# Feed-forward of a two-block layer: five column groups instead of four, the last by token halves, and the context norm moved

## The chip, the cores and the metric

The program runs on one core of one Trainium2 chip. The metric is the device time of one execution in microseconds; three executions of the kernel before gave 4265.05, 4266.02 and 4270.29 us (median 4266.02).

## The reference, cut to what matters

Two blocks follow each other on 1024 tokens of width 1024; a context of 256 tokens joins in the second. Around the change stand the end of the first block and the start of the second (everything in float32):

```
h2 = layer_norm(x) * (1 + scale2) + shift2
u = h2 @ w_up                                   # 1024 x 5632
up = pad(u, two tokens in front)
u = conv_b + sum(conv_w[t] * up[:, t:t + S] for t in range(3))
u_gate, u_val = split(u, 2)                     # 2816 each
f = gelu(u_gate) * u_val
x = layer_norm(ALPHA * x + gate2 * (f @ w_down)) * ln2_g + ln2_b
...
# second block, first layer
n_l = rmsnorm(x, norm_w) * (1 + scale) + shift          # 1024 tokens
n_c = rmsnorm(ctx, norm_w) * (1 + scale_c) + shift_c    # 256 context tokens
y_l, y_c = even_layer(n_l, n_c, ...)                    # begins with n_l, n_c @ w_in
```

The convolution runs along the tokens, so a token needs the two tokens before it.

## The kernel before, in words

Every float32 matrix product is made of three passes over a high and a low part of both factors: `mm3` (L215) issues the three matmuls of lines 217, 218 and 219. Activations with channels in partitions are held as a pair of tiles `hhi`, `hlo` (`alloc_hT`, L221): index 0 holds tokens 0 to 511, index 1 tokens 512 to 1023, index 2 the context. There is one buffer for each index, so a new tile of index 0 can be written only when all readers of the old one are done.

`ffn` (L694) walks over 22 column tiles of 128 hidden channels in four groups of 6, 6, 6 and 4 (L703). For each group, `up` (L710) takes two tiles at a time: it loads the two 256-column slices of `w_up` (gate and value) with `wcols` (L180, split into high and low by ScalarE and VectorE, L176 and L177; two raw buffers, three of high and low each), and for each tile and half accumulates both token halves into a two-bank PSUM tile `p2` (two buffers). ScalarE (L731) and VectorE (L732, L734) convolve 1024 tokens at once, ScalarE applies gelu, GpSimd multiplies (L741), ScalarE and VectorE split the product into `fh` and `fl` (L742, L743). `down` (L746) multiplies the group's tiles by `w_down` for a token tile of 128 and half of the output columns, into PSUM tiles `pj` and `pt` in turn (two of each here, set by `open_ps(2)` at L632). For the first three groups the sum so far is kept in DRAM: for each of 16 (column half, token tile) items a 256 KB piece `xl` is loaded (two buffers), VectorE multiplies by the gate (L770) and adds (L771), and SyncE's queue stores it (L773).

The last group is different (L776 to L805). All of its `up` comes first; then both halves of `w_down`, multiplied by the gate on GpSimd (L173); then for each of the 8 token tiles: load the sum so far into `x2t` (L789, four buffers), two products and adds (L792), layer norm (L794: VectorE statistics, GpSimd power, ScalarE scale), times `ln2_g` on GpSimd (L795), plus `ln2_b` on VectorE (L796), store to DRAM (L803), root-mean-square norm (L804), and `to_hT` (L805, L364), which transposes the tile by TensorE into a `p2` tile and applies scale and shift from there, `ta` (7) of 8 slices on ScalarE (L387), the rest on VectorE (L389), then casts (L390) and subtracts (L391) into `nT[0]` or `nT[1]`. Tiles 6 and 7 take two VectorE operations (L801, L802) in place of L794 to L796.

`ctx_norm` (L1039) then does the same norm for two tiles of the context, writes `nT[2]`, and stores `nT[1]` and `nT[2]` to DRAM for later. `rw_prep1` (L1084) goes on with products of all three token sets with `even_w_in`: `fm_psum` (L1057) accumulates tokens 0 to 511, then 512 to 1023, in one `p2` tile, then the context in a `pj` tile. From here on weights are loaded on SyncE's queue (L1089).

The order of the instructions on each engine is not written by hand: a planner at build time walks over the program with simulated times, takes the earliest written instruction that is ready, and gives out buffers as they come free. On the chip each engine, and each DMA queue, works strictly in that order. All scratch pools stack on one side of the on-chip memory, so a pool opened after another was closed takes over its place and its waits.

## Time and profile before

| | us |
|---|---|
| three timed executions, median (lowest to highest) | 4266.02 (4265.05 to 4270.29) |
| the profiled execution, its own time | 4259.52 |
| its span in the trace | 4257.7 |
| TensorE busy in the span | 3895.7 (91%) |
| VectorE / ScalarE / GpSimd busy | 1964.8 / 1402.8 / 1133.4 |
| mean granted TensorE clock | 0.928 of full speed |

PE is TensorE, PEld its weight loads, DVE VectorE, ACT ScalarE, POOL GpSimd, SP SyncE; an engine's name with a q behind it is its queue of DMA issues. Times in a row count from the start of the span. In rows of the timeline the first number is the start, the second the duration (several merged ones together where the end says xN), and what stands in brackets is the idle time before it and what ended it. Busy times of PE overlap a little from one matmul to the next, so the distance of starts is the better measure of a matmul's price.

### The profile page before, as it was taken

How to read it: one execution, taken by the hardware profiler on the slowest of the kernel's cores; microseconds unless marked ns; L12 is line 12 of the kernel's file. 1: busy time of each engine (PE TensorE's matmuls, PEld its weight loads, DVE VectorE, ACT ScalarE, POOL GpSimd, SP SyncE). 2: the span in 40 equal slices, each digit the busy share in tenths (PEclk: the TensorE clock that was granted, in tenths of full speed). 3: DMA queues.
4: the chain of work that ended last, by engine and by line, in shares of the span. 5: the costliest groups of instructions: out<-in, count | busy, mean ns of one | idle time of the engine just before them, and what ended most of it. 6: DMA issues, size and time to landing. Idle time of an engine off the chain costs nothing. (4 is left out here: it accounts for less than half of the span.)

```text
span 4257.7 us, 62518 instructions
## 1 busy us (share of the span) xinstructions
PE 3895.7 (91%) x24873; PEld 3154.0 (74%) x24873; DVE 1964.8 (46%) x2944; ACT 1402.8 (33%) x2881; POOL 1133.4 (27%) x1135
## 2 busy tenths in 40 slices
PE   7999999988999999789879899988789999998987
PEld 4788877776878788567777787777567877776776
DVE  4232433447343434544235445443566426653576
ACT  4333322215212122442235444353224224432211
POOL 1110302223101011202265333226530200003574
PEclk9999979998999999878989899896789999998998
DMA  5321217573142413332476645553764644324465
GB/s 200 122 95 68 92 58 258 198 271 123 52 138 70 144 54 125 121 133 115 145 245 174 184 135 153 174 155 96 237 203 143 228 135 116 104 73 152 153 200 201
DMA packets 474212, 622.00 MB, mean 146 GB/s; under 512 B 163201, under 2 KB 324403, under 8 KB 467776
## 3 DMA queue, kind: packets, MB, share of 16 engines
q1 hardware_dynamic: 423440, 416.26, 30.4%
q0 software_dynamic: 50480, 201.75, 14.3%
q8 instruction: 196, 3.21, 0.3%
q14 instruction: 96, 0.79, 0.1%
HBM read 423.34 MB, written 193.88 MB: 145 GB/s over the span
## 5 line engine op out<-in xcount | busy, mean ns | idle before, releaser
L217 PE MATMUL p<-hhi,whi 128*128 128x512 f32 x1056 | 416.1, 395 | 5.8 <-DVE hf L389 5.7
L218 PE MATMUL p<-hlo,whi 128*128 128x512 f32 x1056 | 414.3, 392 | 4.3 <-DVE hlo L391 4.3
L219 PE MATMUL p<-hhi,wlo 128*128 128x512 f32 x1056 | 414.1, 392 | 0.0
L217 PE MATMUL pf<-whi,hhi 128*128 128x512 f32 (+1 forms) x992 | 357.7, 362 | 16.8 <-DMA whi<-wkh 6.9
L218 PE MATMUL pf<-wlo,hhi 128*128 128x512 f32 (+1 forms) x992 | 352.7, 356 | 7.9 <-POOL wlo L177 4.9
L219 PE MATMUL pf<-whi,hlo 128*128 128x512 f32 (+1 forms) x992 | 350.4, 354 | 0.0
L176 ACT CAST whi<-wraw 128x2048 fp32r<-128x2048 f32 (+1 forms) x123 | 193.1, 1574 | 463.4 <-PE pt L219 174.8
L177 DVE TENSOR_TENSOR wlo<-wraw,whi 128x2048 fp32r<-128x2048 f32 (+1 forms) x103 | 213.0, 2069 | 275.5 <-ACT whi L176 275.4
L217 PE MATMUL pf<-hhi,whi 128*128 128x512 f32 (+1 forms) x640 | 252.2, 394 | 3.8 <-ACT hyo L2050 1.5
L219 PE MATMUL pf<-hhi,wlo 128*128 128x512 f32 (+1 forms) x640 | 249.7, 390 | 1.8 <-DMA wlo<-wkl 1.8
L218 PE MATMUL pf<-hlo,whi 128*128 128x512 f32 (+1 forms) x640 | 249.8, 390 | 0.0
L217 PEld LDWEIGHTS p<-hhi,whi 128*128 128x128 f32 x1056 | 200.6, 190 | 53.8 <-DVE hf L389 6.1
L217 PEld LDWEIGHTS pf<-whi,hhi 128*128 128x128 f32 x992 | 198.2, 200 | 54.5 <-issue 12.4
L218 PEld LDWEIGHTS p<-hlo,whi 128*128 128x128 f32 x1056 | 200.3, 190 | 46.4 <-DVE hlo L391 5.3
L217 PE MATMUL pj<-whi,hhi 128*128 128x512 f32 (+1 forms) x560 | 216.2, 388 | 19.9 <-ACT whi L176 12.2
L219 PEld LDWEIGHTS p<-hhi,wlo 128*128 128x128 f32 x1056 | 200.1, 189 | 42.8 <-issue 0.8
L219 PE MATMUL pj<-whi,hlo 128*128 128x512 f32 (+1 forms) x560 | 214.2, 384 | 11.2 <-DVE hlo L381 11.2
L218 PEld LDWEIGHTS pf<-wlo,hhi 128*128 128x128 f32 x992 | 198.6, 200 | 34.2 <-POOL wlo L177 5.8
L218 PE MATMUL pj<-wlo,hhi 128*128 128x512 f32 (+1 forms) x560 | 214.9, 384 | 0.3 <-DVE wlo L177 0.3
L219 PEld LDWEIGHTS pf<-whi,hlo 128*128 128x128 f32 x992 | 197.8, 200 | 23.3 <-issue 2.3
L217 PEld LDWEIGHTS pf<-hhi,whi 128*128 128x128 f32 x640 | 122.3, 191 | 35.7 <-issue 9.3
L218 PEld LDWEIGHTS pf<-hlo,whi 128*128 128x128 f32 x640 | 122.2, 191 | 28.9 <-issue 6.9
(762 smaller groups left out, 8677.1 us busy)
## 6 DMA issues: line engine op xcount, KB each, us to landing
wraw<-w_in POOLq DMA_DIRECT2D x25, 1024.0 KB, 5.7
wraw<-w_ada POOLq DMA_DIRECT2D x24, 1024.0 KB, 8.0
wraw<-w_up POOLq DMA_DIRECT2D x22, 1024.0 KB, 6.0
whi<-wkh POOLq DMA_DIRECT2D x40, 512.0 KB, 4.9
wlo<-wkl POOLq DMA_DIRECT2D x40, 512.0 KB, 4.8
wraw<-ada_w POOLq DMA_DIRECT2D x32, 512.0 KB, 4.6
ox<-x SPq DMA_DIRECT2D x48, 256.0 KB
xp<-xl SPq DMA_DIRECT2D x48, 256.0 KB
```

Of the source, the lines that this page charges most:

```text
L176: nc.scalar.copy(hi[:, :n], raw[:, :n])
L177: self.we.tensor_sub(lo[:, :n], raw[:, :n], hi[:, :n].bitcast(F32))
L217: mm(out, L[0], R[0], start=first, stop=False)
L218: mm(out, L[0], R[1], start=False, stop=False)
L219: mm(out, L[1], R[0], start=False, stop=last)
```

## The change

The groups become 6, 6, 4, 4 and 2. The last group of two tiles no longer uses `up` and `down`: it goes through the tokens in two halves, and does for each half all of up, convolution (512 tokens at a time; the last two tokens of the first half are kept in `ends`), down, norms and transposes before the next. The first half's up goes into `p2` tiles, the second's into `pj` (gate) and `pt` (value). `w_down`'s two tiles of rows come as one gated piece of 1024 columns. `ta` is 5 from here on, so three of eight slices go to VectorE. The context norm stands in the fourth group, between its up and its down, writes its result to DRAM, and a new `ctx_load` reads it back where `ctx_norm` stood, and stores `nT[1]`.

```diff
--- before.py
+++ after.py
@@ -700,7 +700,7 @@
         self.nw2 = self.cols_of([a["norm_w_2"][0], a["norm_w_2"][1]], 8, "nw2")
         self.x2_d = [dr.tile([P, D], F32, name=f"x2_{t}") for t in TL]
         self.mod_e = None
-        groups = [(0, 6), (6, 6), (12, 6), (18, 4)]
+        groups = [(0, 6), (6, 6), (12, 4), (16, 4), (20, 2)]
         with ExitStack() as es:
             cp = es.enter_context(self.pool("ffc"))
             cw = self.cols_of([a["conv_w"][0], a["conv_w"][1], a["conv_w"][2], a["conv_b"]], 44, "cvw", cp)
@@ -759,6 +759,8 @@
                     dst = [dr.tile([P, D], F32, name=f"xp{gi}_{t}") for t in TL]
                     with self.pool(f"fff{gi}") as fp, self.pool(f"ffu{gi}") as p:
                         up(p, fp, fs, j0, n)
+                        if gi == 3:
+                            self.ctx_norm()
                         for c in range(2):
                             cs = slice(512 * c, 512 * c + 512)
                             W = self.wcols(w_down, 512 * c, 512, nk=n, k0=j0)
@@ -773,36 +775,78 @@
                                 nc.sync.dma_start(dst[t][:, cs], xl)
                     src = dst
                     continue
-                fp = es.enter_context(self.pool("fffl"))
-                with self.pool(f"ffu{gi}") as p:
-                    up(p, fp, fs, j0, n)
-                with self.pool("ffl") as p:
+                Wg = self.wcols(w_up, j0 * P, 256)
+                Wv = self.wcols(w_up, 2816 + j0 * P, 256)
+                W = self.wcols(w_down, 0, 1024, nk=n, k0=j0, gate=gate2)
+                with self.pool("fffl") as fp, self.pool("ffl") as p:
+                    ends = fp.tile([P, 2, 2, 2], F32, name="fce")
                     g1 = p.tile([P, D], F32, name="ln2g")
                     nc.sync.dma_start(g1, bcast_rows(a["ln2_g"], D))
                     b1 = p.tile([P, D], F32, name="ln2b")
                     nc.sync.dma_start(b1, bcast_rows(a["ln2_b"], D))
-                    W = [self.wcols(w_down, 512 * c, 512, nk=n, k0=j0, gate=gate2[:, 512 * c:512 * c + 512]) for c in range(2)]
-                    nT = [self.alloc_hT(0), self.alloc_hT(1)]
-                    for t in TL:
-                        xx = p.tile([P, D], F32, name="x2t", tag="x2t", bufs=4)
-                        nc.sync.dma_start(xx, src[t])
-                        for c in range(2):
-                            cs = slice(512 * c, 512 * c + 512)
-                            nc.vector.tensor_add(xx[:, cs], xx[:, cs], down(fs, W[c], t, n))
-                        ...
+                    nT = [None, None]
+                    self.ta = 5
+                    for b in range(2):
+                        fs = []
+                        for e in range(2):
+                            ts = []
+                            ps = self.p2() if b == 0 else None
+                            for half, Wu in ((0, Wg), (1, Wv)):
+                                u = ps[:, 512 * half:512 * half + 512] if b == 0 else (self.pt if half else self.pj)()
+                                for k in range(KD):
+                                    wk = (Wu[k][0][:, e * P:e * P + P], Wu[k][1][:, e * P:e * P + P])
+                                    self.mm3(u, wk, (h2T[b][0][:, k, :], h2T[b][1][:, k, :]), k == 0, k == KD - 1)
+                                jj = j0 + e + 22 * half
+                                w = lambda i: cw[:, i, jj:jj + 1]
+                                t = p.tile([P, 512], F32, name="cvh", tag="cvh", bufs=4)
+                                nc.scalar.activation(t, u, AF.Identity, bias=w(3), scale=w(2))
+                                nc.vector.scalar_tensor_tensor(t[:, 1:], u[:, :511], w(1), t[:, 1:], op0=OP.mult, op1=OP.add)
+                                nc.vector.scalar_tensor_tensor(t[:, 2:], u[:, :510], w(0), t[:, 2:], op0=OP.mult, op1=OP.add)
+                                x = ends[:, e, half]
+                                if b == 0:
+                                    nc.vector.tensor_copy(x, u[:, 510:512])
+                                else:
+                                    nc.vector.scalar_tensor_tensor(t[:, 0:2], x, w(0), t[:, 0:2], op0=OP.mult, op1=OP.add)
+                                    nc.vector.scalar_tensor_tensor(t[:, 0:1], x[:, 1:2], w(1), t[:, 0:1],
+                                                                   op0=OP.mult, op1=OP.add)
+                                if half == 0:
+                                    nc.scalar.activation(t, t, AF.Gelu)
+                                ts.append(t)
+                            fh, fl = [fp.tile([P, 512], F32R, name="fh" + x, tag="fh" + x, bufs=4) for x in "hl"]
+                            nc.gpsimd.tensor_mul(ts[0], ts[0], ts[1])
+                            nc.scalar.copy(fh, ts[0])
+                            nc.vector.tensor_sub(fl, ts[0], fh.bitcast(F32))
+                            fs.append((fh, fl))
+                        nT[b] = self.alloc_hT(b)
+                        for t in range(4 * b, 4 * b + 4):
+                            xx = p.tile([P, D], F32, name="x2t", tag="x2t", bufs=4)
+                            nc.sync.dma_start(xx, src[t])
+                            s = slice(t % 4 * P, t % 4 * P + P)
+                            for c in range(2):
+                                cs = slice(512 * c, 512 * c + 512)
+                                self.nq += 1
+                                ps = self.pj() if self.nq % 2 else self.pt()
+                                for k in range(n):
+                                    self.mm3(ps, (fs[k][0][:, s], fs[k][1][:, s]), tuple(x[:, cs] for x in W[k]),
+                                             k == 0, k == n - 1)
+                                nc.vector.tensor_add(xx[:, cs], xx[:, cs], ps)
+                            ...
             self.nT = nT
 
     def swa(self, qkv_d, yb_d):
@@ -1037,22 +1081,29 @@
     NC5 = 1280
 
     def ctx_norm(self):
         nc, a = self.nc, self.a
         me = self.mod_e
-        hc = self.alloc_hT(2)
+        self.nT_d = [None, None, [self.dr.tile([P, KD, 256], F32, name=f"nTd2{x}") for x in "hl"]]
         with self.pool("cxn") as p:
             for i in range(2):
-                x = p.tile([P, D], F32, name="cx", tag="cx", bufs=2)
+                x = p.tile([P, D], F32, name="cx", tag="cx", bufs=1)
                 nc.sync.dma_start(x, a["ctx_2"][i * P:(i + 1) * P, :])
                 self.rms_norm(p, x, x, "cn")
-                self.to_hT(p, x, hc, i, me[:, 1, 8:16], me[:, 1, 0:8])
+                hc = [p.tile([P, KD, P], F32R, name="cxT" + e, tag="cxT" + e, bufs=1) for e in "hl"]
+                self.to_hT(p, x, hc, 0, me[:, 1, 8:16], me[:, 1, 0:8])
+                for t, o in zip(hc, self.nT_d[2]):
+                    nc.sync.dma_start(o[:, :, i * P:(i + 1) * P], t.bitcast(F32))
+    def ctx_load(self):
+        nc = self.nc
+        hc = self.alloc_hT(2)
+        for t, o in zip(hc, self.nT_d[2]):
+            nc.sync.dma_start(t.bitcast(F32), o)
         self.nT.append(hc)
-        self.nT_d = [None] * 3
-        for b in (1, 2):
-            hT = self.nT[b]
-            self.nT_d[b] = [self.dr.tile(list(t.shape), F32, name=f"nTd{b}{x}") for t, x in zip(hT, "hl")]
-            for t, o in zip(hT, self.nT_d[b]):
-                nc.sync.dma_start(o, t.bitcast(F32))
+        self.nT_d[1] = [self.dr.tile([P, KD, 512], F32, name=f"nTd1{x}") for x in "hl"]
+        for t, o in zip(self.nT[1], self.nT_d[1]):
+            nc.sync.dma_start(o, t.bitcast(F32))
 
     def fm_psum(self, W, e, m=P):
 
@@ -2661,7 +2712,7 @@
     K.load_consts()
     K.block1_mix()
     K.ffn()
-    K.ctx_norm()
+    K.ctx_load()
     K.rw_prep1()
     K.mixers()
     K.odd_in()
```

## Rows read from the trace of the kernel before

**Rows 1.** The page, part 1: busy time, share of the span, instructions.

```profile
PE 3895.7 (91%) x24873; PEld 3154.0 (74%) x24873; DVE 1964.8 (46%) x2944; ACT 1402.8 (33%) x2881; POOL 1133.4 (27%) x1135
```

**Rows 2.** Windows: length, busy (count) by engine, granted clock, DMA share, GB/s.

```profile
1046.00:1728.60 682.60, 681.74 (x2994) 551.30 (x2991) 273.33 (x245) 155.28 (x124) 90.42 (x62) 1.00 0.29 96
1728.60:1837.45 108.85, 65.36 (x272) 51.62 (x270) 68.97 (x118) 68.08 (x141) 32.38 (x27) 0.76 0.40 139
...
1747.00:1766.00 19.00, 19.00 (x73) 15.10 (x73) 14.96 (x31) 8.16 (x13) 9.69 (x9) 0.87 0.23 92
...
1793.00:1809.00 16.00, 0.14 (x1) 0.00 (x0) 16.00 (x23) 8.84 (x20) 1.71 (x2) 0.61 0.64 226
...
1826.00:1837.40 11.40, 3.94 (x16) 3.14 (x16) 5.63 (x11) 10.79 (x28) 0.76 (x2) 0.50 0.38 128
```

**Rows 3.** Timeline of TensorE, 1690 to 1850 us.

```profile
1696.43 0.40 PE L219 MATMUL p<-hhi,wlo 128*128 128x512 f32 x1
...
1728.40 0.40 PE L219 MATMUL p<-hhi,wlo 128*128 128x512 f32 x1
1728.63 0.39 PE L219 MATMUL pj<-whi,fl 128*128 128x512 f32 x1
...
1736.33 0.40 PE L219 MATMUL pt<-whi,fl 128*128 128x512 f32 x1
...
1746.53 0.79 PE L217 MATMUL pj<-whi,fh 128*128 128x512 f32 x1 [4.46 <-DVE x2t L792]
...
1766.86 1.03 PE L377 MATMUL p<-ident,x2t 128*128 128x128 f32 x8
...
1822.83 1.97 PE L377 MATMUL p<-ident,x2t 128*128 128x128 f32 x8 [0.64 <-ACT x2t L360]
1826.48 1.97 PE L377 MATMUL p<-ident,cx 128*128 128x128 f32 x8 [1.68 <-DVE hf L389]
...
1837.45 0.79 PE L217 MATMUL p<-hhi,whi 128*128 128x512 f32 x1 [5.71 <-DVE hf L389]
...
1844.58 0.39 PE L217 MATMUL p<-hhi,whi 128*128 128x512 f32 x1
```

**Rows 4.** Timeline of VectorE, 1728 to 1850 us.

```profile
1738.98 1.22 DVE L743 TENSOR_TENSOR fl<-cv,fh 128x1024 fp32r<-128x1024 f32 x1 [3.64 <-ACT fh L742]
1745.78 0.69 DVE L792 TENSOR_TENSOR x2t<-x2t,pj 128x512 f32<-128x512 f32 x1 [5.58 <-DMA x2t<-xp]
...
1755.53 3.33 DVE L796 TENSOR_TENSOR x2t<-x2t,ln2b 128x1024 f32<-128x1024 f32 x1
...
1760.24 1.22 DVE L796 TENSOR_TENSOR x2t<-x2t,ln2b 128x1024 f32<-128x1024 f32 x1
...
1776.82 0.69 DVE L792 TENSOR_TENSOR x2t<-x2t,pj 128x512 f32<-128x512 f32 x1 [1.59 <-DMA x2t<-xp]
...
1797.70 0.68 DVE L792 TENSOR_TENSOR x2t<-x2t,pt 128x512 f32<-128x512 f32 x1
```

**Rows 5.** Groups by line, 1729 to 1850 us: count, busy us, mean ns, idle before.

```profile
L177 DVE TENSOR_TENSOR wlo<-wraw,whi 128x2048 fp32r<-128x2048 f32 x3 | 6.9, 2287 | 6.1 <-ACT whi L176 6.1
```

**Rows 6.** Timeline of VectorE, end of the third group's down.

```profile
1622.40 0.69 DVE L771 SCALAR_TENSOR_TENSOR xl<-xl,dtm 128x512 f32<-128x512 f32 x1 [5.42 <-DMA xl<-xp]
...
1646.90 0.69 DVE L771 SCALAR_TENSOR_TENSOR xl<-xl,dtm 128x512 f32<-128x512 f32 x1
```

**Rows 7.** Line 173, whole span: durations in ns, first and last start.

```profile
L173 POOL TENSOR_TENSOR wraw<-wraw,g x2: 4612/4618/4625, 1658.3 to 1684.0; 128x2048 f32<-128x2048 f32 x2
```

**Rows 8.** Timeline of SyncE's queue, 1690 to 1900 us.

```profile
1690.83 42.39 SPq L165 DMA_DIRECT2D wraw<-even_w_in  x3
...
1740.63 1.92 SPq L789 DMA_DIRECT2D x2t<-xp  x4
...
1788.37 3.30 SPq L789 DMA_DIRECT2D x2t<-xp  x2
```

**Rows 9.** The chain that ended last, in order of time.

```profile
2374.70 16.37 DMA hhi<-nTd1h
```

More of the change, by code (lines that the diff above doesn't have):

```diff
@@ new lines, in ffn @@
+                    nT = [None, None]
[44 more added lines that the diff above has]
+                                nc.vector.tensor_add(xx[:, cs], xx[:, cs], ps)
+                            if t < 6:
+                                self.ln_norm(p, xx, xx, "f1", act=True)
+                                nc.gpsimd.tensor_mul(xx, xx, g1)
+                                nc.vector.tensor_add(xx, xx, b1)
+                            else:
+                                mv = self.ln_stats(p, xx, "f1")
+                                r = self.rpow(p, mv[:, 1:2], 1, 1.0, 1e-5, "f1")
+                                nc.vector.scalar_tensor_tensor(xx, xx, mv[:, 0:1], g1, op0=OP.subtract, op1=OP.mult)
+                                nc.vector.scalar_tensor_tensor(xx, xx, r, b1, op0=OP.mult, op1=OP.add)
+                            nc.sync.dma_start(self.x2_d[t], xx)
+                            self.rms_norm_act(p, xx, xx, "f2", act=True)
+                            self.to_hT(p, xx, nT[b], t % 4, self.mod_e[:, 0, 8:16], self.mod_e[:, 0, 0:8], 1.5)
```

12 lines of the change are left out of this document (removed).

## The prediction

> **What bounds the kernel now.** I read the page's busy shares first: PE is busy 91% of the span [rows 1], so only stretches in which PE is not busy can give time. The windows show one around the change [rows 2]: from 1046 to 1728.6 us the feed-forward keeps PE busy 681.7 of 682.6 us at the full clock; from 1728.6 to 1837.45 us it is busy 65.4 of 108.85 us at a mean clock of 0.76. This second stretch is the last group's down, its norms and the context norm. In it DVE (69.0 us) and ACT (68.1 us) are busy less than two thirds each, so no engine is the bound: a chain from token tile to token tile is. PE's timeline [rows 3] has its steps: up ends at 1728.4, PE works on the slices that are ready until 1736.3, waits for the last convolution, then for `x2t`; the last transposes of tokens start at 1822.8, those of the context at 1826.5, and the next stage starts at 1837.45. Its 25th matmul, the first that needs tokens 512 to 1023 (24 matmuls make one accumulation: 8 slices by 3), starts at 1844.58; that instant is my mark.
>
> **The change part by part.**
>
> *PE's work before the tail.* One matmul costs 0.2267 us in up (142 rows from 1696.43 to 1728.40) and 0.2333 us in down (34 rows from 1728.63 to 1736.33) [rows 3]. The work is the same, but two column tiles of up move behind the last group boundary (2 tiles x 2 halves x 2 blocks x 24 = 192 matmuls, 43.5 us), and two tiles of down move ahead of it (8 tokens x 2 x 2 x 3 = 96 matmuls, 22.4 us). With about 1.6 us for 16 context transposes (half of the pair 2 x 1.03 us of [rows 3] to all of it: 1 to 2) the last group begins at 1728.6 - 43.5 + 22.4 + 1.6 = 1709 us if PE stays dense.
>
> *Smaller groups and one more.* Each group writes its sum to DRAM and reads it back by 16 items with two `xl` buffers. Where these transfers bind, an item takes (1646.90 - 1622.40) / 6 = 4.1 us [rows 6]. A group of six tiles gives an item every 18 x 0.2333 = 4.2 us, so today this is just hidden; a group of four gives one every 2.8 us. Two such groups are new. Per group PE could fall behind by 16 x (4.1 - 2.8) = 21 us less what the four `pj` and `pt` tiles hold, 11 us: 10 us, 20 for both; or nothing, where the next group's up fills the wait, since it writes `p2` tiles. The third boundary of today is the nearest row and is dense [rows 2], so I take 5 us: the last group begins at 1714. The context norm's DVE and ACT work here lies beside PE work in a stretch where DVE is busy 40% and ACT 23% of the time [rows 2]; its stores follow on SP behind `xl` transfers. I cost it at nothing; if that cover failed it would be the 11 us that it takes in the tail today (1826.48 to 1837.45 [rows 3]).
>
> *The last group by halves.* The first half's up takes 21.8 us of PE. From the end of the last up matmul (1728.8) to the end of `fl` (1740.2) the convolution chain took 11.4 us for 1024 tokens [rows 3, 4]; for 512 I take half, 5.7 (bounds 5 and 8, as fixed costs don't halve). PE fills it with the second half's up, and then owes: four tokens' down, 48 x 0.2333 = 11.2, their transposes 4 x 1.03 = 4.1 [rows 3], the second half's up 21.8. So PE ends up at 1714 + 21.8 + 11.2 + 4.1 + 21.8 = 1773, the convolution at 1778.5, the first of the last four tokens' products at 1780. Three small edits hide here: the gated piece of `w_down` (4.6 us on POOL [rows 7], then a split of 2.3 us on DVE [rows 5]) beside the first half's up; the first `x2t` loads, which today start at 1740.6 and hold DVE until 1745.8 and PE for 4.46 us [rows 3, 4, 8], also beside that up; and `ends`, a few short DVE instructions.
>
> *The last four tokens.* Today tokens 4 to 7 start their adds between 1776.8 and 1797.7 [rows 4], because only four `x2t` buffers exist and loads wait for the transposes of earlier tokens (the last two are issued from 1788.4 on [rows 8]). After the change the buffers of tokens 0 to 3 come free during the second half's up, so all four can be added by about 1786. A token needs 21 us from its first add (1745.78) to its transposes (1766.86) [rows 3, 4], and by the windows DVE works (69.0 - 6.9 for three weight splits) / 10 = 6.2 us for each of eight tokens and two context tiles [rows 2, 5]. Four tokens then end between 25 + 7 = 32 us (DVE never idle) and 21 + 5 + 3 x 6.2 = 44 us (one behind another) after 1780. The nearest row, the last token's last add at 1797.7 to the mark at 1844.6, holds 47 us with the context's 11 and 7 of the next stage's first half in it: 29 for one token among two. I take 38: tokens 512 to 1023 are complete at 1818.
>
> *After it.* Without the context's transposes the `p2` buffer of an earlier token comes free first, so the 24 matmuls on tokens 0 to 511 (7.1 us today, 1837.45 to 1844.58 [rows 3]) can run ahead of the last token's end; the mark then comes right at 1818. `ctx_load` reads 2 x 1 MB; a 2 MB load of the same kind held the chain for 16.4 us at worst [rows 9], and its cover is the 48 latent matmuls (11 us), or 96. Bounds 0 and 16; I take 2, as `ctx_load` is issued ahead of the `nT[1]` stores. Mark: 1820.
>
> Sum: 1820 - 1844.6 = -25 us. The profiled execution took 4259.5 us (span 4257.7), so 4234.5; it lies 6.5 us below the median of the runs, so 4241 there.
>
> *The clock.* While PE was idle or on few transposes the granted clock was 0.61 and 0.50, that is 1.2 GHz most of the time, and the first matmuls of the next stage still ran slowly [rows 2, 3]. A tail of some 35 us without dense PE work remains, so I count no gain there.
>
> *DVE beside POOL.* One `ln2_b` add took 3.33 us where POOL's multiply was late, another 1.22 us [rows 4]: 2.1 us more. The sum above carries such hits as they fell today. In the second half's up, DVE has convolutions beside the norms, and POOL their products beside the `ln2_g` multiplies, so there can be more of them; this is rival F. The Trainium skill (SBUF — State Buffer, "Who interferes with whom") speaks against the change here: a DVE instruction with two inputs in this memory and a GpSimd instruction that reads it exclude each other, and the later one is fully blocked. The 3.33 us agrees with it, and by it the sum would be F's.
>
> **The rivals.**
>
> *B, the work is only shuffled.* If DVE and ACT in the new stretch have the same idle share as in the old one (DVE 0.63 busy [rows 2]), 8 x 6.2 us of norms, 6.5 us for the second half's convolution (ten 512-wide instructions at about half of 1.22 us [rows 4]) and 4.6 us of weight splits from 1741.5 on take 61 / 0.63 = 97 us: mark 1838.5 + 2, -4 us, 4262. For it: the order is fixed ahead, and DVE idled on DMA and POOL in order. Against: of that idle time the start (no `x2t`) and the `x2t` turn-around go.
>
> *C, SP's queue.* SP works in order, and today it stood 42.4 us at the next stage's weight loads, waiting for raw buffers [rows 8], with the `ln2` and `x2t` loads behind. The new last group holds all three pairs of split buffers, so those loads wait again. If the plan puts one ahead of a token's `x2_d` store, the second norm, which overwrites that tile, waits for the store, DVE and ACT behind it too. Price up to 42 us: 4241 + 42 = 4283. It decides once the stall on the token chain exceeds 25 us. Against: today's 42 us cost PE nothing, which was dense until 1728.6 [rows 2].
>
> *D, the tail closes up.* No `xl` cost (-5), four tokens in 32 us (-6), no load wait (-2): -38, 4228.
>
> *E, a cold last group.* From 1747 to 1766 PE was busy all the time, but after a pause of 4.5 us the mean clock was 0.87 [rows 2, 3]. If PE pauses between halves because the four `pj`/`pt` tiles now serve both up and down, and the 66 us of matmuls there run at that mean, they take 66 / 0.87 - 66 = 10 us more: 4251. The Trainium skill (TensorE: Matmul & The Clock Gate, "Part 1: The HAM clock gate") has the throttled clock as the default that activity releases, and the rows agree.
>
> *F, DVE held by POOL.* If each of the four `ln2_g` multiplies beside the second half's up costs DVE the 2.1 us of the row: 8 us more, 4249.
>
> **How the numbers follow.** Chances: the forecast 0.44 (own range 4230 to 4254), D 0.14, E 0.09, F 0.07, B 0.14, C 0.12. About 0.2%, 8.5 us, is what a measurement of this kernel can tell from no change. Faster is the forecast, D, F and all but 0.01 of E: 0.73; same is B and the rest: 0.15; slower is C: 0.12. The range leaves out C and the ends of D: 4218 to 4270.
>
> **What would show it.** Right: the last `p<-ident,x2t` transposes near 1810 instead of 1822.8; tokens 0 to 3 normed beside PE at full clock; no context transposes after them; the next stage's 25th matmul near 1820; `hhi<-nTd2h` not on the chain. Wrong: PE idle behind `dtm` or `xl` in groups three and four; DVE waiting on `x2t` loads again; a long SP wait at `even_w_in` with `x2_d` stores behind; a wait of the first context product on its load; or a later stage whose order has changed and that gives the time back.

## The result

The changed kernel takes 4307.46 us (median of 4 runs, 4306.09 to 4320.07) where the kernel before, beside it on the same chip, takes 4268.16: a ratio of 1.0093, 95% interval 1.007 to 1.0115. It is slower by some 39 us; forecast were 4241 us and 0.73 for faster. The profiled execution has a span of 4304.3 us, 46.6 more than the one of before.

The page of the changed kernel, its first line and part 1 (compare [rows 1]):

```profile
span 4304.3 us, 62672 instructions
...
PE 3919.8 (91%) x24873; PEld 3168.2 (74%) x24873; DVE 2004.0 (47%) x3013; ACT 1397.2 (32%) x2872; POOL 1127.7 (26%) x1135
```

PE has the same 24873 matmuls and is busy 24.1 us longer for them; DVE has 69 more instructions and 39.2 us more work. The windows of the changed kernel say where the time lies. The first ends at the same instant as in [rows 2]; the second ends at the mark of the prediction, the 25th matmul of the next stage; the third at the store of that stage's first product, `rw_r`; the fourth at the end.

```profile
1046.00:1728.60 682.60, 671.20 (x2918) 540.53 (x2915) 289.03 (x277) 153.36 (x132) 85.20 (x61) 0.98 0.32 107
1728.60:1866.76 138.16, 91.24 (x373) 71.77 (x371) 90.59 (x158) 65.66 (x122) 34.59 (x28) 0.81 0.36 128
1866.76:1924.23 57.47, 53.61 (x287) 46.57 (x285) 21.08 (x29) 15.51 (x16) 0.00 (x0) 0.97 0.43 144
1924.23:4304.30 2380.07, 2133.11 (x16165) 1731.13 (x16164) 1179.44 (x1934) 813.51 (x1828) 810.21 (x829) 0.90 0.51 159
```

The same stretches of the kernel before, from its mark on (1844.58):

```profile
1728.60:1844.58 115.98, 72.49 (x296) 57.38 (x295) 70.26 (x120) 68.67 (x141) 32.38 (x27) 0.76 0.44 157
1844.58:1897.01 52.43, 52.43 (x287) 45.17 (x285) 21.45 (x29) 15.86 (x16) 0.00 (x0) 1.00 0.30 97
1897.01:4257.70 2360.69, 2116.76 (x16165) 1719.16 (x16164) 1179.58 (x1934) 813.78 (x1828) 812.28 (x829) 0.91 0.51 160
```

So the 46.6 us are three losses: 22.2 up to the mark (1866.76 - 1844.58), 5.0 from the mark to the first `rw_r` store, and 19.4 behind it, where the diff touches nothing. In that last stretch the engines have the same instruction counts, PE is busy 16.4 us longer and idle 3.0 longer. This splits one traced execution of each kernel. At the medians the difference is 39.3 us; if the traces' 27.2 up to that store hold there too, some 12 are left behind it (an estimate).

PE's timeline of the changed kernel shows the first loss being built up:

```profile
1679.72 0.80 PE L217 MATMUL pj<-whi,fh 128*128 128x512 f32 x1 [3.05 <-ACT fh L742]
...
1723.62 0.80 PE L217 MATMUL pt<-whi,fh 128*128 128x512 f32 x1 [3.56 <-DVE dtm L772]
...
1733.22 0.39 PE L219 MATMUL pt<-whi,fl 128*128 128x512 f32 x1
...
1738.23 0.39 PE L219 MATMUL p<-hhi,wlo 128*128 128x512 f32 x1
1746.35 0.77 PE L217 MATMUL p<-hhi,whi 128*128 128x512 f32 x1 [7.73 <-DVE fce L810]
...
1757.84 0.77 PE L217 MATMUL p<-hhi,whi 128*128 128x512 f32 x1 [3.86 <-DVE fce L810]
...
1800.61 0.39 PE L219 MATMUL pt<-hhi,wlo 128*128 128x512 f32 x1
...
1844.04 1.97 PE L377 MATMUL p<-ident,x2t 128*128 128x128 f32 x8 [18.46 <-ACT x2t L360]
...
1859.52 0.77 PE L217 MATMUL p<-hhi,whi 128*128 128x512 f32 x1 [1.08 <-DVE hf L389]
...
1866.76 0.39 PE L217 MATMUL p<-hhi,whi 128*128 128x512 f32 x1
```

And VectorE's, in the same stretch:

```profile
1722.08 0.69 DVE L773 SCALAR_TENSOR_TENSOR xl<-xl,dtm 128x512 f32<-128x512 f32 x1 [8.77 <-DMA xl<-xp]
...
1744.60 0.75 DVE L806 SCALAR_TENSOR_TENSOR cvh<-p,cvw,cvh 128x511 f32<-128x511 f32 x1
1745.38 0.75 DVE L807 SCALAR_TENSOR_TENSOR cvh<-p,cvw,cvh 128x510 f32<-128x510 f32 x1
1746.05 0.15 DVE L810 COPY fce<-p 128x2 f32<-128x2 f32 x1
...
1771.77 0.69 DVE L836 TENSOR_TENSOR x2t<-x2t,pj 128x512 f32<-128x512 f32 x1 [1.70 <-PE pj L219]
...
1796.80 4.35 DVE L177 TENSOR_TENSOR wlo<-wraw,whi 128x2048 fp32r<-128x2048 f32 x1 [1.98 <-ACT whi L176]
...
1813.46 0.69 DVE L822 TENSOR_TENSOR fhl<-cvh,fhh 128x512 fp32r<-128x512 f32 x1 [0.76 <-ACT fhh L821]
...
1819.07 0.68 DVE L836 TENSOR_TENSOR x2t<-x2t,pj 128x512 f32<-128x512 f32 x1
...
1833.42 3.31 DVE L845 SCALAR_TENSOR_TENSOR x2t<-x2t,f1mv,ln2g 128x1024 f32<-128x1024 f32 x1
...
1863.55 0.69 DVE L391 TENSOR_TENSOR hlo<-hf,hhi 128x512 fp32r<-128x512 f32 x1 [0.74 <-ACT hhi L390]
```

The row to stop at is the one at 1746.35. In the first half a tile's gate and value are two halves of one `p2` tile. PE had done the gates of both column tiles by 1738.23; the value's matmuls, which write the other half, then waited until DVE had copied the gate's last two columns (line 810). DVE was late with that: it stood behind the fourth group's `xl` transfers and convolved the first gate only at 1744.60. Nothing in the data asks for that wait; the two halves share only the tile.

Most of the second loss, at the start of the next stage, is the queue. SP issues the small constants of that stage (`bon`, `colr`, `a2r`) behind the reload of the context and the stores of `nT[1]` (SyncE's queue, changed kernel):

```profile
1863.54 0.32 SPq L1106 DMA_DIRECT2D nTd1h<-hhi  x1
1864.30 0.32 SPq L1102 DMA_DIRECT2D hhi<-nTd2h  x1
...
1867.25 1.31 SPq L1152 DMA_DIRECT2D bon<-c_bones  x1
...
1869.46 4.38 SPq L1179 DMA_DIRECT2D a2r<-rw_a  x4
```

DVE gets `bon` 16.7 us after its issue:

```profile
1883.98 0.23 DVE L1154 CAST bonr<-bon 128x128 fp32r<-128x128 f32 x1 [19.75 <-DMA bon<-c_bones]
```

and PE waits for `colr`, 3.9 of the 5.0 us; in the kernel before it has no wait from its mark to the first `rw_r` store:

```profile
1884.22 0.23 PE L405 MATMUL pj<-ident,colr 14*128 14x14 f32 x1 [0.98 <-DMA colr<-rw_mu]
1887.33 0.26 PE L405 MATMUL pj<-ident,colr 20*128 20x20 f32 x1 [2.88 <-DMA colr<-rw_a]
```

### The profile page after: what moved, and what is told of

It reads as the page before. It is cut to its first block, busy times and chain, and to the rows that moved or that the text cites. A ratio compares the mean times of both kernels' runs of the same rounds, so it can differ in the third digit from the quotient of the medians.

```text
span 4304.3 us, 62672 instructions
## 1 busy us (share of the span) xinstructions
PE 3919.8 (91%) x24873; PEld 3168.2 (74%) x24873; DVE 2004.0 (47%) x3013; ACT 1397.2 (32%) x2872; POOL 1127.7 (26%) x1135
## 5 line engine op out<-in xcount | busy, mean ns | idle before, releaser
L217 PE MATMUL p<-hhi,whi 128*128 128x512 f32 x1024 | 407.0, 398 | 15.4 <-DVE fce L810 11.6
L218 PE MATMUL p<-hlo,whi 128*128 128x512 f32 x1024 | 405.0, 396 | 4.3 <-DVE hlo L391 4.3
L219 PE MATMUL p<-hhi,wlo 128*128 128x512 f32 x1024 | 403.9, 395 | 0.0
```

The lines of the kernel that those rows point to most:

```text
L217: mm(out, L[0], R[0], start=first, stop=False)
L218: mm(out, L[0], R[1], start=False, stop=False)
L219: mm(out, L[1], R[0], start=False, stop=last)
```

## The experiments

A run is read by two numbers of its trace: when the first `rw_r` store is issued (what the feed-forward, the context and the start of the next stage cost; before 1897.0, changed 1924.2) and how long it takes from there to the end of the span (before 2360.7, changed 2380.1). Two traces of one order lay 2.1 us (before) and 0.6 us (changed) apart at the store, so differences of that size there tell nothing. The ratio is that of all timed executions of a run to those of the kernel before beside them.

| run | first rw_r store | from it to the end | ratio to before, 95% interval |
|---|---|---|---|
| e1_upfirst | 1911.6 | 2376.5 | 1.0066 (1.0042 to 1.0091) |
| e2_ctx | 1914.5 | 2363.5 | 1.0059 (1.0041 to 1.0077) |
| e3_five | 1920.7 | 2378.4 | 1.0066 (1.0043 to 1.0089) |
| e4_ctxold | 1924.0 | 2365.6 | 1.0053 (1.0027 to 1.0078) |
| e7_ctxold_up | 1905.5 | 2368.7 | 1.0045 (1.0026 to 1.0064) |
| e8_xl4 | 1905.2 | 2377.6 | 1.0001 (0.9984 to 1.0018) |
| e9_nob1 | 1903.1 | 2378.6 | 1.0010 (0.9990 to 1.0030) |
| e10_t4 | 1899.2 | 2371.7 | 1.0001 (0.9982 to 1.0020) |
| e11_ctx2 | 1910.3 | 2371.8 | 1.0030 (1.0011 to 1.0048) |
| e12_bt4 | 1897.2 | 2372.3 | 1.0014 (0.9998 to 1.0031) |
| r1_before | 1899.1 | 2358.8 | 1.0000 (0.9976 to 1.0025) |
| r2_after | 1924.8 | 2392.7 | 1.0128 (1.0019 to 1.0237) |

**The wait inside the p2 tile.** Both products of a tile first, then the convolutions:

```diff
+                            us = []
                             for half, Wu in ((0, Wg), (1, Wv)):
                                 u = ps[:, 512 * half:512 * half + 512] if b == 0 else (self.pt if half else self.pj)()
...
+                                us.append(u)
+                            for half, u in enumerate(us):
                                 jj = j0 + e + 22 * half
```

> The changed kernel, but in the last group the gate's and the value's 24 matmuls of a tile are both emitted before either is convolved. In the changed kernel the value's matmuls of the first half waited 7.73 us (at 1746) and 3.86 us (at 1758) for the copy of the gate's last two columns, which reads another half of the same PSUM tile. Theory 1 (that wait, and what DVE does late behind it, carries the local loss of some 28 us): both waits of PE on L810 are gone, the second half's up ends about 11 us earlier (1789 in place of 1800.6), the first rw_r store moves from 1924 to about 1912, and the time falls by as much, to 4290 to 4298. Rival (DVE, full from 1796 to 1843, sets when the last tokens are normed whatever PE does before): the two waits go, the up ends earlier, but the first rw_r store stays within 4 us of 1924 and the time within 0.2% of the changed kernel's. Both leave some 19 us behind the first rw_r store, where the changed kernel took 2380 us to its end and the kernel before 2361.

Measured: the first `rw_r` store moved by 12.6 us to 1911.6, as theory 1 had it. PE's waits between 1715 and 1765 in that run are these three, and none is for line 812, the copy `fce` there:

```profile
1721.58 0.80 PE L217 MATMUL pt<-whi,fh 128*128 128x512 f32 x1 [3.75 <-DVE dtm L772]
...
1750.28 0.50 PE L217 MATMUL pj<-whi,fhh 128*128 128x512 f32 x1 [1.37 <-ACT fhh L823]
...
1756.36 0.50 PE L217 MATMUL pj<-whi,fhh 128*128 128x512 f32 x1 [3.05 <-ACT fhh L823]
```

The order of emission alone made the wait: 12.6 of the 27.2 us lost up to the store.

**The context norm alone, and its old place.** First the kernel before with only the context moved, ahead of the last group's up, by the changed kernel's two functions:

```diff
                 with self.pool(f"ffu{gi}") as p:
+                    self.ctx_norm()
                     up(p, fp, fs, j0, n)
-    K.ctx_norm()
+    K.ctx_load()
```

> The kernel before (four groups, the last with four column tiles and no halves), with the context norm alone moved: it is emitted ahead of the last group's up, stored to DRAM, and loaded after the last token. Theory 1 (the context norm's move is sound and the loss comes from the groups and halves): the 16 context transposes and the norm's vector work leave the stretch before the next stage, the first rw_r store comes 4 to 12 us before the 1897 of the kernel before, time 4252 to 4266. Rival (the loads of the context, the stores of the normed tokens and the next stage's small constants behind them on one queue give it back): the next stage's first context matmul or its small constants come late as in the changed kernel, the first rw_r store is at 1897 or later, time 4268 or more. What lies behind the first rw_r store: 2361 us in the kernel before; if a re-made order alone is enough to cost the 19 us lost there in the changed kernel, it comes out away from 2361 here too, though nothing of those stages is changed.

Measured: the rival; 17.5 us later at the store. But the place is not that of the change, and its own cost is seen first: PE's queue holds the context's transposes ahead of the last up, and they wait for `cx`:

```profile
1651.74 1.94 PE L377 MATMUL p<-ident,cx 128*128 128x128 f32 x8 [17.85 <-DVE cx L346]
1662.00 1.94 PE L377 MATMUL p<-ident,cx 128*128 128x128 f32 x8 [8.32 <-DVE cx L346]
```

because DVE's statistics wait for the load (6.12 us before the row at 1648.13). PE stood idle for these 26.2 us, because in its order the transposes came before dense work; 17.5 us of it arrived at the store. Behind the store the run took 2363.5.

Then the changed kernel with the context norm after the last token again, written to SBUF as in the kernel before:

```diff
-                        if gi == 3:
-                            self.ctx_norm()
-    K.ctx_load()
+    K.ctx_norm()
```

> The changed kernel with the context norm at its old place (after the last token, no trip through DRAM): groups and halves alone. Theory 1 (the move of the context norm is worth what it was before, some 10 us, and the rest is lost by groups and halves): first rw_r store 5 to 12 us later than in the changed kernel, at 1929 to 1936, time about 4315. Rival (the context norm beside the fourth group delays that group, at 1680 to 1693, and the loads delay the next stage, so its move is worth nothing or costs): first rw_r store at 1924 or earlier, time 4307 or less.

Measured: 1924.0, the same as with the move (1924.2): the rival. The windows of 1680 to 1700 say what the move costs in its place. Changed kernel:

```profile
1680.00:1700.00 20.00, 18.55 (x69) 14.33 (x70) 12.58 (x15) 3.68 (x9) 5.04 (x2) 0.77 0.35 116
```

With the context at its old place:

```profile
1680.00:1700.00 20.00, 20.00 (x88) 16.18 (x87) 10.99 (x14) 0.69 (x1) 0.91 (x1) 1.00 0.34 122
```

PE does 69 matmuls where it did 88. This window shows only part of the price. By the time PE had finished the fourth group's down and the 48 gate matmuls of the first half, 15 us had been lost: it got there at 1738.6 with the move and at 1723.3 without it. From 1600 on it had idled 8.3 us against 2.1, at a mean clock of 0.94 against 1.00. Part of this was lost again without the move, because PE only came earlier to the wait inside the `p2` tile (context at its old place):

```profile
1736.74 0.76 PE L217 MATMUL p<-hhi,whi 128*128 128x512 f32 x1 [13.47 <-DVE fce L808]
```

It waited 17.3 us in all at line 808 in place of 11.6, so the last four tokens' first add was 9.6 us earlier (1809.5 against 1819.1). The rest went at the end: PE's wait for the first scaled one of these tokens was 24.1 us in place of 18.5, and the context's transposes stood behind them again, so the next stage began at 1863.6 against 1859.5; there it had no wait for `colr`. With the `p2` wait gone as well:

> Both edits of the runs before it together: gate and value matmuls of a tile emitted ahead of its convolution, and the context norm at its old place. Against the run with the first edit alone (first rw_r store 1911.6, half of it the wait on the gate's columns gone) it tells what the move of the context norm is worth once that wait is gone. Theory 1 (the move is worth nothing here, because the last tokens' chain on DVE and ACT ends last and the context norm fits beside it): first rw_r store within 4 us of 1911.6, time 4270 to 4292. Rival (the move did save some 10 us, which the false wait hid in the changed kernel): first rw_r store at 1918 to 1925, time 4290 to 4305. From the first rw_r store to the end the runs so far took 2361 to 2380 us with the same 16165 matmuls, and what differs is PE's busy time (2117 to 2138), not its idle time (240 to 247): this run is to fall on that line too, some 2125 busy where little of its order differs from the kernel before.

Measured: 1905.5, against 1911.6 with the context moved. So the move of the context norm, free in the prediction, costs 6.1 us net: some 15 beside the fourth group, less what the tail saves. That is 2 us outside theory 1's bound, and on the other side from the rival, which had it save time.

**Five groups without halves.** The kernel before with `groups = [(0, 6), (6, 6), (12, 4), (16, 4), (20, 2)]` and nothing else.

> The kernel before with five groups of 6, 6, 4, 4 and 2 column tiles in place of 6, 6, 6 and 4, the last one still by whole tokens and the context norm at its old place. Theory 1 (a fifth group costs little while PE is full): PE waits behind xl and dtm of the fourth group for 5 to 15 us, but the last group's up is half as long and its two column tiles' convolution has 24 fewer matmuls beside it; first rw_r store at 1900 to 1915. Rival (the short group itself loses: DVE, which evacuates the fourth group's down, convolves late, and PE has nothing else): first rw_r store at 1915 to 1930, as late as with halves, and time 4285 to 4310. The order behind the first rw_r store is re-made here too: 2361 us to the end as before, or up to 2380.

Measured: 1920.7, at the lower end of the rival's range: the five groups alone lose 23.7 us. Its last up matmul starts at 1759.12, 30.7 us after that of the kernel before [rows 3]: PE's timeline of this run.

```profile
1759.12 0.40 PE L219 MATMUL p<-hhi,wlo 128*128 128x512 f32 x1
1759.36 0.39 PE L217 MATMUL pj<-whi,fh 128*128 128x512 f32 x1
...
1769.67 0.80 PE L217 MATMUL pj<-whi,fh 128*128 128x512 f32 x1 [7.36 <-ACT fh L742]
```

22.4 of the 30.7 are, by the forecast's price, the 96 down matmuls that the change moves ahead of the last group. In the kernel before they ran inside the tail, where PE has time to spare; ahead of it they delay it by their full length, and from the last up matmul to the store the run is only 7.0 us shorter for having less PE work (161.6 us for 168.6). That the chain of the tail is the reason is read from the traces; no run moves the 96 matmuls alone. Against this run the halves give 15.2 us where neither the `p2` wait nor the moved context is in the way (1920.7 to 1905.5).

**The xl buffers.** On top of e7_ctxold_up:

```diff
-                                xl = p.tile([P, 512], F32, name="xl", tag="xl", bufs=2)
+                                xl = p.tile([P, 512], F32, name="xl", tag="xl", bufs=2 if gi < 2 else 4)
-                                tm = p.tile([P, 512], F32, name="dtm", tag="dtm", bufs=1)
+                                tm = p.tile([P, 512], F32, name="dtm", tag="dtm", bufs=1 if gi < 2 else 2)
```

> The same, with four xl buffers in place of two and two dtm buffers in place of one in the third and fourth group. Theory 1 (the short groups' evacuation is held by the round trip of xl through two buffers: DVE waited 27 us for xl loads at 1640 to 1760, and convolves the last group's first tile 7 us after it is there): DVE's waits for xl fall under 10 us, the first half's first convolution comes 8 to 12 us earlier, the first rw_r store 6 to 12 us earlier than without the buffers, time 4262 to 4280. Rival (the stretch after the second half's adds, bound by DVE and ACT, and the loads' queue set the end): xl waits fall but the first rw_r store moves by less than 4 us.

Measured: DVE's wait for `xl` loads fell from 22.4 to 12.9 us, the store moved by 0.3 us: the rival. The evacuation of the short groups, for which the prediction took 5 us, is not what ends last. What does is seen in this run at the last four tokens, on PE:

```profile
1822.25 3.38 PE L377 MATMUL p<-ident,x2t 128*128 128x128 f32 x16 [23.37 <-ACT x2t L360]
```

on ACT:

```profile
1805.15 2.50 ACT L333 ACTIVATE x2t<-x2t,f1m,f_r 128x1024 f32<-128x1024 f32 x2 [4.33 <-DVE f1m L332]
1814.67 0.63 ACT L355 ACTIVATE f2sq<-x2t 128x512 f32<-128x512 f32 x1 [7.02 <-DVE x2t L840]
```

and on POOL:

```profile
1806.47 5.62 POOL L839 TENSOR_TENSOR x2t<-x2t,ln2g 128x1024 f32<-128x1024 f32 x2 [4.18 <-ACT x2t L333]
```

The four tokens' adds run from 1792.4 to 1800.3, all four; their statistics follow, all four; the first ACT scaling is at 1805.15, the first square at 1814.67, the first transpose at 1822.25. One token's path has become the path of four abreast, step by step, and PE has nothing from 1800 to 1820.

**Work or length of the chain?** DVE is busy 19.85 of those 20 us, so the cause could be its amount of work. Two edits on the run with four `xl` buffers, for which the two readings expect different times: taking DVE work out (line `nc.vector.tensor_add(xx, xx, b1)` left out), and putting DVE work in but steps of POOL and ACT out (`if t < 6` becomes `if t < 4`).

> The run with four xl buffers, with the addition of the layer norm's bias left out for tokens 0 to 5 (that part of the computation is missing here). It takes six DVE instructions of 1.2 us out, four of them (tokens 0 to 3) from the stretch in which the second half is convolved, two from the last tokens' chain. In that run DVE was busy for 74 us of 1760 to 1840 while PE had nothing from 1800 to 1820. Theory 1 (DVE's amount of work sets when the last tokens come out): the first rw_r store, at 1905.2 there, comes 5 to 8 us earlier. Rival (the length of the last four tokens' chain sets it: adds, statistics, scaling on ACT, multiplication on POOL, addition, squares, scaling, each for all four tokens before the next): only the one or two additions on the chain count, 1 to 3 us earlier.

> The run with four xl buffers, with tokens 4 and 5 normed as tokens 6 and 7 are: two DVE instructions of some 1.25 us in place of one ACT scaling, one POOL multiplication (2.8 us) and one DVE addition. It adds some 2.7 us of work to DVE and takes the two POOL steps and the ACT step out of the last four tokens' chain, and the hold on DVE while POOL multiplies (2.07 us for 1.27 in that run). Theory 1 (DVE's amount of work sets the end): first rw_r store at 1905 to 1909, not earlier. Rival (the chain's length sets it): 4 to 9 us earlier, 1896 to 1901, and PE's one long wait for a scaled token (23.4 us) shrinks by as much; time 4266 to 4272, at or a little below the kernel before.

Measured: 7.3 us less work on DVE gives 2.1 us, no more than two traces of one order differ by, and not the 5 to 8 of theory 1; 2.7 us more work on DVE, with a shorter chain, gives 5.9 (1905.2 to 1899.2). Both lie in the rival's ranges: the length of the chain sets the end. (From 1760 to 1840 the windows give 64.6 us of DVE work in the run with four `xl` buffers, not the 74 that the expectation names.) PE's longest wait for a scaled token falls from 23.37 to 16.62 us. The same edit in the kernel before is the counter-test:

> The kernel before with tokens 4 and 5 normed on DVE as 6 and 7 are, nothing else. Theory 1 (the six us that this gave with halves came from all four last tokens going through the chain together, one POOL step and one ACT step longer; in the kernel before they come one after the other, each hidden behind the next): first rw_r store within 2 us of 1897. Rival (the two POOL and ACT steps hold the last tokens there as well): 3 to 6 us earlier. Behind the store the order is re-made: 2361 to 2380 us.

Measured: 1897.15, 0.1 us from the kernel before: theory 1. There tokens come one behind the other, and one token's POOL and ACT steps lie beside another's.

**The context norm one group earlier**, with the first edit and `t < 4`:

```diff
-                        if gi == 3:
-                            self.ctx_norm()
+                        if gi == 2:
+                            while self.mod_e is None:
+                                try:
+                                    next(mods)
+                                except StopIteration as e:
+                                    self.mod_e = e.value
+                            self.ctx_norm()
```

> The changed kernel with three edits: gate and value matmuls of a tile ahead of its convolution; tokens 4 and 5 normed on DVE as 6 and 7 are; the context norm one group earlier, beside the third group's down, where PE has the fourth group's up behind it (xl buffers are two, as in the changed kernel). With the context at its old place and four xl buffers the first rw_r store was at 1899.2. Theory 1 (the context's statistics and scalings on DVE lengthen the last tokens' chain by some 6 us, and the move lost in the changed kernel only because it stood beside the fourth group, where PE waits on DVE anyway): first rw_r store at 1890 to 1896. Rival (a context norm beside any four-tile group delays that group's evacuation, and PE, full there, loses as much as the chain gains; or the reload and the small constants behind it start the next stage late): 1899 to 1908.

Measured: 1910.3, a little behind the rival's range. The transposes at 1533 and 1547 cost PE no wait here, but the first tokens' adds begin at 1760.5 (1742.9 in e10_t4, which has the context at its old place and four `xl` buffers), and the waits for `colr` behind the reload are back (3.9 us). Why the adds begin 17.6 us later is only partly seen: from 1500 on PE waited 6.6 us for `cv`, `fh` and `dtm`, where e10_t4 had none of these waits, and 10.1 us in place of 7.0 for the first half's product.

**Behind the first rw_r store.** All eleven kernels whose later stages were ordered anew, the changed one among them, took longer there in their trace than the kernel before: 2363.5 to 2380.1 us for the same 16165 matmuls. A trace is one execution, though, and those of one kernel differ by as much (the kernel before, beside the first runs: 4249.3 to 4277.4 us in 23 executions). So the last column of the table does not rank the orders. e7_ctxold_up and e8_xl4 show it: their stores lie 0.3 us apart, and by the traces the second is the longer behind it, by 8.9 us; but the traced execution was the fastest of ten for the one and the slowest of ten for the other. At the medians e8_xl4 is the faster, 4275.3 against 4289.0 us, and the intervals of the two ratios do not touch. A re-made order alone can thus be worth some 14 us here. For the changed kernel, both kernels were traced once more:

> The kernel before once more, unchanged, for a second trace of the same order. From the first rw_r store to the end it took 2361 us, and in ten other kernels, whose later stages hold the same instructions in a re-made order, 2364 to 2380. Theory 1 (the order sets that stretch): within 4 us of 2361, with PE busy for 2113 to 2121 us of it. Rival (the chip grants the clock anew in each execution, whatever the order): anywhere from 2361 to 2380.

> The changed kernel once more, unchanged. Theory 1 (the order sets the stretch behind the first rw_r store): within 4 us of 2380, PE busy for 2129 to 2137 us of it. Rival (the clock is granted anew in each execution): anywhere from 2361 to 2380. In both the first rw_r store is at 1924, within 3 us.

Measured: 2358.8 for the kernel before, theory 1 (with PE busy for 2107.7 us of it, a little under the range named); 2392.7 for the changed kernel, above the ranges of both theories and 12.6 us from its own first trace. In both pairs of traces the changed kernel is the longer there, and the execution adds its own part. Where it lies can be read from two lines of the mixers, whose first and last matmul stand at the end of a group's answer (kernel before, lines 1826 and 1478):

```profile
L1826 PE MATMUL p<-wS,wrr x640: 218/218/366, 2287.3 to 2978.8; 64*64 64x64 f32 x160
L1478 PE MATMUL pj<-ident,eya x320: 218/218/367, 3016.6 to 3157.3; 64*64 64x64 f32 x160
```

Changed kernel (lines 1877 and 1529):

```profile
L1877 PE MATMUL p<-wS,wrr x640: 218/218/366, 2316.5 to 3019.4; 64*64 64x64 f32 x160
L1529 PE MATMUL pj<-ident,eya x320: 218/218/367, 3051.0 to 3206.5; 64*64 64x64 f32 x160
```

From the first of the one to the last of the other are 870.0 us before and 890.0 after; 871.6 and 911.2 in the second traces. The windows of these stretches, kernel before (first trace), and changed kernel (first trace, then the second one):

```profile
2287.30:3157.30 870.00, 772.06 (x9003) 640.67 (x9005) 428.81 (x858) 359.83 (x920) 363.41 (x491) 0.88 0.57 168
```

```profile
2316.50:3206.50 890.00, 787.48 (x9003) 653.85 (x9005) 427.95 (x858) 360.23 (x920) 361.46 (x491) 0.86 0.55 164
```

```profile
2311.80:3223.00 911.20, 804.01 (x9003) 665.77 (x9005) 425.26 (x858) 360.27 (x920) 359.88 (x491) 0.84 0.54 160
```

The same 9003 matmuls keep PE busy for 772, 787 and 804 us while DVE, ACT and POOL need nearly the same time in all three, and the mean granted clock falls: PE ran more of them at 1.2 GHz. If the clock had only its two levels, 2 x (1 - 0.88) x 870 = 209 us lay at the lower one before, 2 x (1 - 0.86) x 890 = 249 us after and 2 x (1 - 0.84) x 911 = 292 in the second trace. This is an estimate, and some of that time PE was idle. What was measured is that of the 20.0 and 41.2 us by which the stretch grew against the kernel before's first trace, 15.4 and 32.0 are PE's busy time and the rest is idle. The clock is not the only way to lose there: behind the store e12_bt4 has PE busy for 2118.6 us, as the kernel before (2116.8), at the same mean clock of 0.91, and took 11.6 us longer, 9.8 of it idle. That this stage's streams are woven in another order is seen in the traces (of the 16165 matmuls behind the store, only 11244 have the same tiles at the same place of PE's order in both kernels). Which change of place opens which pause was not traced, and stays open.

## Why the prediction was wrong, step by step

The mark was forecast at 1820 and came at 1866.76, 46.8 us late. The last four tokens' first add was 39.1 us late (1819.1 for 1780): PE ended the second half's up at some 1801 instead of 1773, chiefly because the context norm was not free (some 14 us) and because of a wait that the forecast does not have (11.6 us), and the convolution behind it was 7.8 us longer than its term. The four tokens then took 7 us more than theirs. Behind the mark came 3 us more than the forecast's 2, and some 12 (medians) to 19 us (traces) from a stage that the change does not touch. The first term, PE's work before the tail, was right: with the context norm at its old place PE's 1723.3 counts back to a start at 1712.4, for 1714.

- *Start of the last group, 1714, and the first half's up, 21.8 us.* The fourth group's down ended at 1733.2, with 48 of the first half's 96 up matmuls done by 1738.2; counted back, that is a start at 1727.6. The term that failed is the context norm "at nothing": it set PE back by 15 us at this point, and its stated price without cover, 11, was the better one. PE's sum and the few us for `xl` held: with the context back, the `p2` wait gone and four `xl` buffers the first half's tokens begin at 1745.1, for 1741.5 forecast.
- *The `p2` wait* was not in the list at all: the text names `p2` tiles as something that up may fill and transposes may take, not as tiles whose halves wait for each other. It took 11.6 us of PE and 12.6 at the `rw_r` store, and with it fell "PE fills it with the second half's up": PE stood at the value first.
- *Second half's convolution, 5.7 us (5 to 8).* From the last up matmul (1800.61) to the end of `fl` (1814.15) it took 13.5. DVE had the first half's norms and two weight splits (4.35 and 2.28 us) in the same queue; the step had the convolution alone.
- *The last four tokens, 38 us (32 to 44).* From the first add (1819.07) to the end of the last split (1864.2), 45; and they began at 1819 instead of 1780. The mechanism was taken from one token's path plus DVE's share per token; the four went through it abreast. The loads of `x2t`, the part that was expected to give the time, did not hold anything: no add of these tokens waited for one. The 24 matmuls on tokens 0 to 511 did not run ahead of the tokens' end, as forecast, but from 1859.5, behind the last transposes, so the mark came 2.5 us after the last split.
- *Rival C (SP's queue)* did not come: the `even_w_in` issues of the stretch took 0.38 us each.
- *Rival F (DVE held by POOL)* came in small, and not beside the second half's up, where the four `ln2b` additions took 1.21 to 1.23 us, but at the last tokens: lines 845 and 846 took 3.31 and 3.36 us once each, where 1.28 and 1.27 were their other times. The Trainium skill (SBUF — State Buffer, "Who interferes with whom") says that such a DVE instruction and a reading GpSimd instruction exclude each other. The 3.31 and 3.36 agree: POOL's `ln2_g` multiplications ran at 1833.17 and 1837.11, just ahead of both. In e10_t4 POOL is left out of tokens 4 and 5, so a part of its 5.9 us may come from there; no run parts it.
- *Rival B (only shuffled, 4262)* is the best description of e10_t4: without the `p2` wait, without the moved context, with four `xl` buffers and `t < 4` it stands at 1.0001 (0.9982 to 1.0020) of the kernel before, its next stage starting at 1839.3 for 1837.45 [rows 3]. For the change as made, no rival had the price.
- *Behind the mark*, `ctx_load` was sized 2 us (0 to 16); mark to `rw_r` store cost 5.0 more than before, 3.9 of it by the small constants queued behind the load and not by the context product.
- *A later stage whose order changed* stood in the last list as a thing that gives time back. It is 19.4 of the 46.6 us between the traces (some 12 of 39.3 at the medians) and had no chance and no price in the range. What in the new order costs this time stays open. The Trainium skill (TensorE: Matmul & The Clock Gate, "Part 1: The HAM clock gate") describes a clock that is throttled by default and released by activity; the mixers' rows agree in direction: with PE idle for 97.9, 102.5 and 107.2 us of the stretch the mean clock was 0.88, 0.86 and 0.84. Only runs could size it.

In sum, at the `rw_r` store, in the order in which the runs part them: five groups +23.7 (1897.0 to 1920.7), halves -15.2 (1905.5), the moved context +6.1 (1911.6), the `p2` wait +12.6 (1924.2). The last two depend on the order of the steps: with the `p2` wait put back first it is +18.5 (1905.5 to 1924.0), and the moved context then adds 0.2. The forecast's terms for five groups, 22.4 + 5, are near the first, though it gave no price for five groups without halves. To reach -25 the halves with the context out of the tail had to give some 52 us, and they gave 15.2 - 6.1 = 9.1 where nothing stood in their way.

## What to carry to other kernels

Emit all matmuls that write one PSUM tile before the first reader of any part of it, or give each part a tile of its own; look for this wherever a tile is filled in pieces. Work of a busy engine that is moved ahead of a tail bound by another chain can delay that tail by its full length (here 22.4 us of it went with 23.7 at the store); and four items that enter a chain of three engines together go through it abreast, so count the chain's steps, not one item's path. And where a planner orders the whole program, price the untouched stages from several re-made orders, each by the median of many executions and not by one trace, before crediting a local gain of 20 us.

## What the runs showed of the hardware

The same instructions in another order kept TensorE busy 15 to 32 us longer in one stage of 870 us (772.06 us before, 787.48 and 804.01 in two executions after, for 9003 matmuls), at mean granted clocks of 0.88, 0.86 and 0.84. Two executions of one order lay 1.6 us apart in that stage for the kernel before (870.0 and 871.6) and 21.2 for the changed one (890.0 and 911.2). Across kernels that differ in order alone behind the `rw_r` store, medians of ten executions differed by 13.6 us where the stores lay 0.3 us apart (e7_ctxold_up and e8_xl4). A VectorE instruction on two 128x1024 float32 tiles took 1.27 and 1.28 us alone, and 3.36 and 3.31 where a GpSimd multiplication had started just before it.
